# A two-layer diffusion backbone step: splitting the first FFN weights during the output projection, other FFN pass sizes in layer 1, and the gate transposes at the end

## The chip, the cores and the metric

The kernel runs on one core of one Trainium2 chip. The metric is the device time of one execution in microseconds (us). The core has five engines that work side by side: TensorE (PE, matmuls, with its weight loads as PEld), VectorE (DVE), ScalarE (ACT), GpSimd (POOL) and SyncE (SP), which here issues all DMAs in one queue, in order. Every engine runs its instructions in a fixed order and waits on semaphores; an instruction that waits holds up all that stand behind it on its engine.

## The reference

One inference step of two layers over 1152 tokens (1024 latent, 128 context) of width 1024. In each layer an input projection feeds three mixers (latent attention, an mLSTM and a gated linear recurrence), and then:

```
mix = jnp.concatenate([a_out, m_out, g_out], axis=-1) @ lp['w_out']
x = layernorm(ALPHA * x + g1 * mix, lp['ln1_g'], lp['ln1_b'])
h2 = x * (1 + sc2) + sh2
gate, up = jnp.split(h2 @ lp['w_ffn_in'], 2, axis=-1)
x = layernorm(ALPHA * x + g2 * ((jax.nn.silu(gate) * up) @ lp['w_ffn_out']), lp['ln2_g'], lp['ln2_b'])
```

The FFN is 2816 wide, which is 22 blocks of 128. The vectors sh, sc and g come from `silu(c) @ w_mod + b_mod`, for each layer and for two kinds of token. All of it is float32.

## The kernel before

**Number format.** Every matmul is done in three products of split operands: a value is held as hi (an ACT cast, L150, for weights L145) and lo (source minus hi, L151 or L146, on DVE or POOL), and hi·hi, lo·hi and hi·lo are added in PSUM (L155 to L157). A "unit" is a weight tile of 128x1024: a DMA into a raw buffer (L144), hi (L145), lo (L146). The raw buffers are a ring, `r_raw`, and a load waits until the buffer that it takes is free.

**Phases.** Each of the layers 0 and 1 runs phase A (input projection), B (mixers), C (output projection), D (FFN). Tokens are worked in 9 tiles of 128, n=0 to 8.

- *Phase C* takes a tile n through 48 matmuls of 128x512. DVE multiplies by the gate row (L1394) and adds ALPHA·x (L1395), where x was loaded at L1385 into a ring of three buffers, `rx` (in layer 1 DVE first multiplies and adds rows to x, L1387 and L1388). Then comes the layer norm: DVE statistics (L1322 to L1324), a power on POOL (L1325), DVE (L1333), an ACT scaling (L1334). `next_h` transposes the tile on PE (8 transposes, L1342), empties the two banks by ACT (L1347) and DVE (L1349), splits the result into `hhi` and `hlo`, and stores three differences of its quarters in DRAM, `sex` (L1354 to L1359). The normed x goes to DRAM as well, `sx` (L1399, or L1403 behind two POOL operations, L1401 and L1402, in layer 0).
- *`ffn_in`* computes gate and up in seven products p1 to p7 for each of the 22 blocks, a Strassen scheme over 2x2 quarters (matmuls at L1449). Each product has two parts q (token tiles 0 to 4 and 5 to 8). p1, p5, p2 and p3 use hhi and hlo; p6, p7 and p4 use three tiles `ex` that are loaded back from sex (L1536) and split (L1537 and L1538). A block's weights are loaded (L1454, L1455), summed on DVE (L1466, L1472 to L1474) and split into seven pairs. The ring of x and other buffers of phase C are given back at its end, and the ex tiles take memory that phase C has held.
- *`ffn_out`* works in three passes over the 22 blocks: 9, 8 and 5 blocks in both layers (`PASSES`). In each pass a tile n loads its hidden values (L1596) and runs 6 matmuls of 128x512 for each block: 54, 48 and 30. Pass 0 leaves its sum in `acc`, pass 1 adds (L1613), multiplies by the gate (POOL, L1618) and adds ALPHA·x (DVE, L1619), where x, `xr`, was loaded at L1600 into a buffer of `r_raw`. Pass 2 adds the rest (L1615 on DVE, L1616 on DVE or POOL), and the layer norm follows. In layer 1 the last rows (L1634, L1635) and the store of the output (L1636) come behind it. The units of passes 0 and 1 are kept in the memory of hhi and hlo (`home`, nine slots), those of pass 2 in five more (`tail`). In layer 0, passes 0 and 1 also compute next layer's modulation, three vectors a tile (`mod_gemv`, L211 to L213: a load into `r_raw`, and two DVE operations of 128x1024), and `gsave` (L225 to L227) transposes two gates on PE and stores them through one buffer, `gT`.

**Order.** A scheduler decides in which order the instructions stand on each engine. It knows the program's dependencies and a model of the durations; on the chip the order is then fixed.

## Time and profile before

| | us |
|---|---|
| three runs: median (lowest, highest) | 3640.34 (3639.33, 3640.81) |
| the profiled execution, its own time | 3641.28 |
| its span, first to last instruction | 3639.5 |
| PE busy in the span | 3405.9 (94%) |
| DVE, POOL, ACT busy | 2264.8, 1988.8, 1635.7 |
| output projection of layer 0, last matmul | 1033.9 |
| output projection of layer 1, last matmul | 2810.6 |
| FFN output of layer 0, pass 1 into pass 2 | about 1765 |
| FFN output of layer 1, first and last matmul | about 3324 and 3621.7 |

The times in the rows below are us from the start of the span. In a timeline row the bracket at the end is how long the engine was idle just before, and what it waited for. The granted clock of PE (PEclk) is 1.00 at its higher level, 2.4 GHz, and 0.50 at its lower one, 1.2 GHz.

### The profile page before, as it was taken

What the parts mean: (1) busy time and instruction counts of PE and PEld (TensorE: products, weight loads), DVE (VectorE), ACT (ScalarE), POOL (GpSimd) and SP (SyncE); (2) the same over time, 40 slices, a digit from 0 to 9 for tenths busy, and PEclk for the clock granted to TensorE, in tenths of its full rate; (3) what the DMA queues carried; (4) which work ended last, traced back from release to release, by engine and by line L of the source; (5) the groups of instructions that cost most, each with busy time, mean ns of one, the idle gap of its engine ahead of it and who ended that gap; (6) DMA issues with size and microseconds to landing.
All of it is one profiled execution on the core that took longest, in us unless ns stands there. A gap on an engine that the chain in (4) does not pass through costs nothing. (4 is left out here: it accounts for less than half of the span.)

```text
span 3639.5 us, 56085 instructions
## 1 busy us (share of the span) xinstructions
PE 3405.9 (94%) x20556; PEld 3034.6 (83%) x20556; DVE 2264.8 (62%) x4492; ACT 1635.7 (45%) x2877; POOL 1988.8 (55%) x1745
## 2 busy tenths in 40 slices
PE   7999987999989999999889989989999999999997
PEld 7998875776779999988689888877767899998875
DVE  6868878555674444487775678765558544443246
ACT  4264564887343333312272636577853433333211
POOL 3455566777665555401453556567863555552176
PEclk9899976999989999999999999789999999999998
DMA  6212153002352222375422021401044322224222
GB/s 244 72 40 43 39 167 100 18 21 81 121 160 85 85 85 85 111 252 179 156 79 62 30 45 34 137 25 25 22 132 139 110 73 73 73 74 139 94 99 80
DMA packets 331272, 335.77 MB, mean 92 GB/s; under 512 B 191458, under 2 KB 270386, under 8 KB 330996
## 3 DMA queue, kind: packets, MB, share of 16 engines
q1 hardware_dynamic: 330996, 332.19, 29.5%
q8 instruction: 161, 2.64, 0.3%
q14 instruction: 115, 0.94, 0.1%
HBM read 263.54 MB, written 68.56 MB: 91 GB/s over the span
## 5 line engine op out<-in xcount | busy, mean ns | idle before, releaser
L151 POOL TENSOR_TENSOR t<-t,t 128x512 fp32r<-128x512 f32 (+3 forms) x318 | 437.8, 1378 | 374.8 <-ACT t L150 374.4
L150 ACT CAST t<-t 128x512 fp32r<-128x512 f32 (+5 forms) x404 | 270.7, 673 | 698.0 <-PE bank L1449 278.7
L1449 PE MATMUL bank<-hhi,t 128*128 128x256 f32 (+1 forms) x2816 | 570.8, 295 | 12.4 <-DVE t L1349 11.5
L155 PE MATMUL bank<-hhi,t 128*128 128x384 f32 (+1 forms) x1220 | 455.1, 378 | 19.2 <-ACT t L150 5.1
L157 PE MATMUL bank<-hhi,t 128*128 128x384 f32 (+1 forms) x1220 | 460.0, 378 | 8.8 <-DVE t L151 8.8
L1449 PEld LDWEIGHTS bank<-hhi,t 128*128 128x128 f32 x2816 | 456.2, 189 | 13.6 <-ACT t L150 12.3
L156 PE MATMUL bank<-hlo,t 128*128 128x384 f32 (+1 forms) x1220 | 460.9, 378 | 4.9 <-POOL hlo L151 4.1
L1187 POOL TENSOR_TENSOR t<-t,t 128x512 fp32r<-128x512 f32 (+1 forms) x304 | 383.3, 1281 | 125.4 <-ACT t L1186 103.0
L1449 PE MATMUL bank<-t,t 128*128 128x320 f32 (+1 forms) x3168 | 434.2, 297 | 2.3 <-DVE t L1507 1.7
L1449 PEld LDWEIGHTS bank<-t,t 128*128 128x128 f32 x3168 | 427.9, 190 | 3.7 <-DVE t L1507 1.9
L1449 PE MATMUL bank<-hlo,t 128*128 128x320 f32 (+1 forms) x1408 | 415.2, 295 | 0.0
L155 PE MATMUL bank<-t,hhi 128*128 128x256 f32 (+3 forms) x1232 | 386.8, 315 | 12.1 <-DVE t L1107 5.4
L156 PE MATMUL bank<-t,hhi 128*128 128x256 f32 (+3 forms) x1232 | 388.0, 315 | 4.3 <-POOL t L146 4.3
L157 PE MATMUL bank<-t,hlo 128*128 128x256 f32 (+3 forms) x1232 | 388.4, 316 | 0.3 <-POOL hlo L151 0.3
L155 PEld LDWEIGHTS bank<-hhi,t 128*128 128x128 f32 x1220 | 237.9, 196 | 57.3 <-ACT t L150 6.7
L1137 DVE TENSOR_REDUCE t<-bank 128x1 f32<-128x384 f32 (+1 forms) x400 | 203.9, 538 | 122.6 <-PE bank L1136 119.5
L157 PEld LDWEIGHTS bank<-hhi,t 128*128 128x128 f32 x1220 | 240.1, 197 | 39.2 <-DVE t L151 12.1
L156 PEld LDWEIGHTS bank<-hlo,t 128*128 128x128 f32 x1220 | 239.6, 196 | 34.7 <-POOL hlo L151 5.1
L1449 PEld LDWEIGHTS bank<-hlo,t 128*128 128x128 f32 x1408 | 265.4, 188 | 0.3 <-issue 0.2
L155 PEld LDWEIGHTS bank<-t,hhi 128*128 128x128 f32 x1232 | 239.8, 195 | 30.2 <-DVE t L1107 5.6
L213 DVE SCALAR_TENSOR_TENSOR t<-t,t 128x1024 bf16<-128x1024 f32 x176 | 239.3, 1359 | 40.6 <-DMA t<-in_w_mod_dram 31.6
L156 PEld LDWEIGHTS bank<-t,hhi 128*128 128x128 f32 x1232 | 240.4, 195 | 20.1 <-POOL t L146 4.7
(355 smaller groups left out, 7329.1 us busy)
## 6 DMA issues: line engine op xcount, KB each, us to landing
t<-in_w_mod_dram SPq DMA_DIRECT2D x96, 512.0 KB
t<-in_w_ffn_in_dram SPq DMA_DIRECT2D x88, 512.0 KB
t<-in_w_ffn_out_dram SPq DMA_DIRECT2D x44, 512.0 KB
t<-in_w_in_dram SPq DMA_DIRECT2D x40, 512.0 KB
shid<-t SPq DMA_DIRECT2D x88, 160.0 KB
sx<-t SPq DMA_DIRECT2D x27, 512.0 KB
t<-sx SPq DMA_DIRECT2D x27, 512.0 KB
shid<-t SPq DMA_DIRECT2D x88, 128.0 KB
```

The source lines that it names most:

```text
L150: self.nc.scalar.copy(hi, src)
L151: (eng or self.nc.gpsimd).tensor_tensor(lo, src, hi.bitcast(F32), op=ALU.subtract)
L155: mm(ps, a[0], b[0], start=first, stop=False)
L156: mm(ps, a[0], b[1], start=False, stop=False)
L157: mm(ps, a[1], b[0], start=False, stop=last)
L213: nc.vector.scalar_tensor_tensor(junk, raw, 1.0, cB[s], op0=ALU.mult, op1=ALU.mult, accum_out=self.modfm[:, l, j, s:s + 1])
L1137: V.tensor_reduce(nm[:, i, b:b + 1] if i < 8 else nm[:, i, 3:4], ps, axis=AX.X, op=ALU.max, negate=True)
L1187: G.tensor_tensor(pl, e, ph.bitcast(F32), op=ALU.subtract)
L1449: mm(ps, a[x][:, k * P:(k + 1) * P], view(y, k, n0, n1), start=first and k == 0 and i == 0, stop=k == 3 and i == 2, skip_group_check=True)
```

## The change

The first block's weights of `ffn_in` were loaded, summed and split behind the output projection; now a generator, `ffn_weights`, is taken one step further at each of the tiles n=5 to 8 of phase C, so that a11, the first sum sA, a12 and sC are split there. For that phase C and `ffn_in` share the rings `r_raw` (four buffers instead of phase C's own three), `rS` and four of the nine pairs of `rA`, and phase C gives up memory: `rx` has two buffers instead of three, `ru` one instead of two. In `next_h` the split into hhi and hlo stands ahead of the last two differences. In layer 1 the FFN output passes have 5, 8 and 9 blocks; pass 0 has its units in `home[0:5]`, pass 1 in `home[5:9]` and four of `tail`, pass 2 in all of `home`. In layer 0 the modulation vectors, 48 in all, were worked three a tile, 27 in pass 0 and the rest at the tiles n=0 to 6 of pass 1; now pass 1 has three a tile up to n=4 and two a tile for n=5 to 7. Both `gsave` come at the end of `ffn_out`.

```diff
-PASSES = ((0, 9), (9, 17), (17, KF))
+PASSES = (((0, 9), (9, 17), (17, KF)), ((0, 5), (5, 13), (13, KF)))
+PRE = 4
...
+        V.tensor_tensor(e[:, 1], b22, b12, op=ALU.subtract)
+        V.tensor_tensor(b12, b12, b11, op=ALU.subtract)
+        self.split(self.hhi[:, :, c], self.hlo[:, :, c], t3, V if n == 8 else None)
+        V.tensor_tensor(e[:, 0], b22, b12, op=ALU.subtract)
+        V.tensor_tensor(e[:, 2], b21, e[:, 0], op=ALU.subtract)
...
-            self.r_raw = z.ring(3, [P, U])
...
-            rx = z.ring(3, [P, D])
+            rx = z.ring(2, [P, D])
...
-            rt, ru = z.ring(2, [P, D]), z.ring(2, [P, D])
+            rt, ru = z.ring(2, [P, D]), z.ring(1, [P, D])
...
+                if n == 4:
+                    gen = self.ffn_weights(l, 0, rS, rA)
+                elif n > 4:
+                    next(gen)
...
+            self.r_raw = z.ring(4, [P, U])
...
+                rS = zi.ring(3, [P, 512])
+                rA = Ring([[zi([P, 512], F32R) for _ in range(2)] for _ in range(PRE)])
...
+    def ffn_weights(self, l, j, rS, rA):
...
+        def sp(src):
+            s = rA.next()
+            self.split(s[0], s[1], src, V if j == 0 else G)
+            out.append(s)
+
+        V.tensor_tensor(sA, a21, a22, op=ALU.add)
+        for src in (a11, sA):
+            sp(src)
+            yield out
+        V.tensor_tensor(sB, sA, a11, op=ALU.subtract)
+        V.tensor_tensor(sC, a12, sB, op=ALU.subtract)
+        V.tensor_tensor(a21, a11, a21, op=ALU.subtract)
+        for src in (a12, sC, sB, a22, a21):
+            sp(src)
+            yield out
...
-        tail = [(z([P, U], F32R), z([P, U], F32R)) for _ in range(PASSES[2][1] - PASSES[2][0])]
+        tail = [(z([P, U], F32R), z([P, U], F32R)) for _ in range(4 if last else 5)]
...
+        slots = [home[0:5], home[5:9] + tail, home] if last else [home, home, tail]
+        for i, (j0, j1) in enumerate(PASSES[l]):
+            w = [self.unit(ins["w_ffn_out"][l, j * P:(j + 1) * P, :], slot=slots[i][j - j0],
+                           eng=V if i == 0 or not last and i == 1 or last and i == 2 and j - j0 > 4 else G) for j in range(j0, j1)]
...
-                for g in (16, 40):
-                    self.gsave(1, g, r_t.next())
...
+                now = 0 if i == 1 and n == 8 else 2 if i == 1 and n > 4 else 3
+                for m in mods[:now]:
...
+        if not last:
+            for g in (16, 40):
+                self.gsave(1, g, r_t.next())
```

In the changed file the lines of `next_h` stand one further down, those of phase C five to six (L1395 becomes L1401), those of `ffn_out` some twelve (L1618 becomes L1630).

**First place: ACT behind the output projection of layer 1.** Rows of the order on ACT, before the change. The casts of shape 128x4x320 are hi of the ex tiles (L1537) and wait for their loads; L1334 is the norm's scaling, L1347 empties a bank of transposes, L150 into hhi follows it.

```order
L1334 ACTIVATE t_25063<-t_25063,t_25087 128x1024
L150 CAST t_26054<-t_25938 128x512
L1347 ACTIVATE t_25071<-bank_68,t_25095,t_25091 128x128 x4
L1537 CAST t_25950<-t_25954 128x4x320
L150 CAST hhi_76<-t_25071 128x8x128
L1334 ACTIVATE t_25059<-t_25059,t_25083 128x1024
L1537 CAST t_25958<-t_25962 128x4x320
L1347 ACTIVATE t_25067<-bank_66,t_25095,t_25091 128x128 x4
```

The same stretch of the changed kernel, where these are L1548, L1335, L1348 and L151:

```order
L1548 CAST t_25961<-t_25965 128x4x320
L1335 ACTIVATE t_25081<-t_25081,t_25101 128x1024
L1335 ACTIVATE t_25085<-t_25085,t_25105 128x1024
L151 CAST hhi_76<-t_25089 128x8x128
L1348 ACTIVATE t_25089<-bank_66,t_25113,t_25109 128x128 x4
L1548 CAST t_25969<-t_25973 128x4x320
L151 CAST hhi_76<-t_25089 128x8x128
L1335 ACTIVATE t_25081<-t_25081,t_25101 128x1024
L1348 ACTIVATE t_25089<-bank_68,t_25113,t_25109 128x128 x4
L151 CAST hhi_76<-t_25089 128x8x128
L1548 CAST t_25977<-t_25981 128x4x320
L1348 ACTIVATE t_25089<-bank_66,t_25113,t_25109 128x128 x4
```

Before, one scaling (n=8) stands behind the first ex cast; now those of n=6 and 7 do, that of n=8 stands behind the second, and emptying the bank of n=8 behind the third.

**Second place: POOL from pass 1 into pass 2 of layer 0's FFN output.** Before the change; L146 is lo of a unit of pass 2, in the order of its raw buffers u0, u1, u4, u2, u3.

```order
L146 TENSOR_TENSOR t_14740<-t_9766,t_14736 128x1024
L1618 TENSOR_TENSOR t_14776<-t_14776,t_14780 128x1024
L146 TENSOR_TENSOR t_14748<-t_9770,t_14744 128x1024
L146 TENSOR_TENSOR t_14772<-t_9766,t_14768 128x1024
L1618 TENSOR_TENSOR t_14776<-t_14776,t_14780 128x1024
L146 TENSOR_TENSOR t_14756<-t_9758,t_14752 128x1024
L146 TENSOR_TENSOR t_14764<-t_9762,t_14760 128x1024
```

After it (L147 and L1630), in the order u1, u0, u2, u4, u3:

```order
L147 TENSOR_TENSOR t_14726<-t_8774,t_14722 128x1024
L147 TENSOR_TENSOR t_14718<-t_8770,t_14714 128x1024
L147 TENSOR_TENSOR t_14734<-t_8762,t_14730 128x1024
L1630 TENSOR_TENSOR t_14754<-t_14754,t_14758 128x1024
L147 TENSOR_TENSOR t_14750<-t_8770,t_14746 128x1024
L147 TENSOR_TENSOR t_14742<-t_8766,t_14738 128x1024
```

Before, u0 stood ahead of the multiplication of n=7, and u1 and u4 between it and that of n=8; now that of n=7 stands ahead of all units, and u1, u0 and u2 ahead of that of n=8.

**Third place: SP from pass 1 into pass 2 of layer 1's FFN output.** Before the change; L1600 is the load of xr (here n=8), L144 a unit of pass 2, L1596 a tile's hidden values.

```order
L1600 DMA t_25938<-sx_92 128x1024
...
L1596 DMA t_30846<-shid_119 128x640
L144 DMA t_25942<-in_w_ffn_out_dram 128x1024
...
L144 DMA t_25942<-in_w_ffn_out_dram 128x1024
L1596 DMA t_30850<-shid_119 128x640
L144 DMA t_25946<-in_w_ffn_out_dram 128x1024
L1596 DMA t_30846<-shid_119 128x640
L144 DMA t_25934<-in_w_ffn_out_dram 128x1024
L1596 DMA t_30850<-shid_119 128x640
L144 DMA t_25938<-in_w_ffn_out_dram 128x1024
```

After it (L1612, L145 and L1608), with nine units in the order u0, u4, u1, u8, u5, u2, u6, u3, u7:

```order
L1612 DMA t_24917<-sx_92 128x1024
...
L1608 DMA t_30799<-shid_122 128x1152
L145 DMA t_24921<-in_w_ffn_out_dram 128x1024 x2
L1608 DMA t_30803<-shid_122 128x1152
L145 DMA t_24925<-in_w_ffn_out_dram 128x1024
L145 DMA t_24921<-in_w_ffn_out_dram 128x1024
L145 DMA t_24925<-in_w_ffn_out_dram 128x1024
L1608 DMA t_30799<-shid_122 128x1152
L145 DMA t_24913<-in_w_ffn_out_dram 128x1024 x2
L1608 DMA t_30803<-shid_122 128x1152
L145 DMA t_24917<-in_w_ffn_out_dram 128x1024 x2
```

In both, the last load of a unit takes the buffer that held xr of n=8 (t_25938 before, t_24917 now). Before, one of five units did; now two of nine do, one behind the other.

## Rows read from the trace of the kernel before

**Rows 1.** The page, part 1: busy time, share and instructions.

```profile
PE 3405.9 (94%) x20556; PEld 3034.6 (83%) x20556; DVE 2264.8 (62%) x4492; ACT 1635.7 (45%) x2877; POOL 1988.8 (55%) x1745
```

**Rows 2.** Windows: stretch, length, busy time (instructions) by engine, granted clock, DMA share, GB/s.

```profile
1010.00:1034.00 24.00, 24.00 (x113) 19.56 (x112) 16.52 (x33) 8.76 (x14) 17.52 (x10) 1.00 0.45 136
2750.00:2770.00 20.00, 20.00 (x96) 16.36 (x95) 18.97 (x32) 7.30 (x13) 7.39 (x4) 1.00 0.41 122
1725.00:1765.00 40.00, 36.56 (x158) 28.90 (x156) 38.45 (x52) 3.88 (x4) 9.67 (x4) 1.00 0.61 202
1765.00:1795.00 30.00, 18.45 (x55) 12.53 (x55) 12.24 (x8) 6.38 (x7) 18.21 (x9) 0.83 0.30 103
3323.90:3525.00 201.10, 199.89 (x865) 163.60 (x866) 64.77 (x50) 36.26 (x43) 64.78 (x27) 0.99 0.30 99
3525.00:3570.00 45.00, 32.67 (x109) 24.49 (x108) 14.85 (x12) 8.15 (x9) 21.25 (x9) 0.81 0.23 81
3570.00:3610.00 40.00, 40.00 (x178) 33.14 (x177) 30.09 (x50) 8.96 (x10) 38.79 (x31) 1.00 0.26 88
3610.00:3622.00 12.00, 9.55 (x41) 7.25 (x39) 11.56 (x16) 2.67 (x3) 9.44 (x8) 1.00 0.23 87
```

**Rows 3.** Timeline of PE around the ends of both output projections.

```profile
1033.91 0.40 PE L157 MATMUL bank<-t,hlo 128*128 128x512 f32 x1
...
1045.41 1.97 PE L1342 MATMUL bank<-ident,t 128*128 128x128 f32 x8 [8.46 <-ACT t L1334]
1054.42 0.60 PE L1449 MATMUL bank<-hhi,t 128*128 128x320 f32 x1 [7.04 <-DVE t L1349]
...
2810.58 0.40 PE L157 MATMUL bank<-t,hlo 128*128 128x512 f32 x1
...
2829.51 0.61 PE L1449 MATMUL bank<-hhi,t 128*128 128x320 f32 x1 [4.49 <-DVE t L1349]
```

**Rows 4.** Timelines of SP and ACT: first ex load and its cast, both layers.

```profile
1034.34 0.57 SPq L1536 DMA_DIRECT2D t<-sex  x1
...
1039.91 1.26 ACT L1537 CAST t<-t 128x1280 fp32r<-128x1280 f32 x1 [3.16 <-DMA t<-sex]
...
2811.20 1.42 SPq L1536 DMA_DIRECT2D t<-sex  x2
...
2819.65 1.26 ACT L1537 CAST t<-t 128x1280 fp32r<-128x1280 f32 x1 [4.93 <-DMA t<-sex]
```

**Rows 5.** Timeline of DVE behind layer 0's output projection.

```profile
1041.20 1.49 DVE L1538 TENSOR_TENSOR t<-t,t 128x1280 fp32r<-128x1280 f32 x1 [1.98 <-ACT t L1537]
...
1046.97 3.28 DVE L1538 TENSOR_TENSOR t<-t,t 128x1280 fp32r<-128x1280 f32 x1 [2.89 <-ACT t L1537]
1050.18 2.82 DVE L1466 TENSOR_TENSOR t<-t 128x512 f32<-128x512 f32 x1
1052.92 1.35 DVE L1349 TENSOR_SCALAR t<-bank,t,t 128x128 f32<-128x128 f32 x4
```

**Rows 6.** Timelines of DVE, SP and POOL in layer 0's FFN output, pass 1 into 2.

```profile
1778.41 3.34 DVE L1619 SCALAR_TENSOR_TENSOR t<-t,t 128x1024 f32<-128x1024 f32 x1 [2.33 <-POOL t L1618]
...
1781.78 0.34 SPq L144 DMA_DIRECT2D t<-in_w_ffn_out_dram  x1
...
1786.78 2.36 POOL L146 TENSOR_TENSOR t<-t,t 128x1024 fp32r<-128x1024 f32 x1 [6.11 <-ACT t L145]
```

**Rows 7.** Timeline of DVE in layer 0's FFN output, the last modulation operation.

```profile
1761.12 1.22 DVE L213 SCALAR_TENSOR_TENSOR t<-t,t 128x1024 bf16<-128x1024 f32 x1
```

**Rows 8.** Timelines of DVE, SP and PE in layer 1's FFN output, pass 1 into 2.

```profile
3556.60 1.23 DVE L1619 SCALAR_TENSOR_TENSOR t<-t,t 128x1024 f32<-128x1024 f32 x1 [2.48 <-POOL t L1618]
...
3557.85 0.33 SPq L144 DMA_DIRECT2D t<-in_w_ffn_out_dram  x1
...
3562.32 2.01 PE L155 MATMUL bank<-t,t 128*128 128x512 f32 x4 [3.05 <-ACT t L145]
```

**Rows 9.** Timeline of DVE behind the last matmul.

```profile
3630.43 0.68 DVE L1615 TENSOR_TENSOR t<-bank,t 128x512 f32<-128x512 f32 x1
```

More of the change, by code (lines that the diff above doesn't have):

```diff
@@ L1350, in next_h, with phase_c @@
         t3 = tmp.rearrange("p (k t) -> p k t", k=KD)
-        if e is not None:
-            V, G = nc.vector, nc.gpsimd
-            b11, b12, b21, b22 = [t3[:, 4 * i:4 * i + 4, 64 * j:64 * j + 64] for i in range(2) for j in range(2)]
-            V.tensor_tensor(e[:, 1], b22, b12, op=ALU.subtract)
-            V.tensor_tensor(b12, b12, b11, op=ALU.subtract)
-            V.tensor_tensor(e[:, 0], b22, b12, op=ALU.subtract)
-            V.tensor_tensor(e[:, 2], b21, e[:, 0], op=ALU.subtract)
-            for i in range(3):
-                nc.sync.dma_start(self.s_ex[i][:, :, n * 64:(n + 1) * 64], e[:, i])
-        self.split(self.hhi[:, :, c], self.hlo[:, :, c], t3, nc.vector if e is not None and n == 8 else None)
-    def phase_c(self, l):
+        if e is None:
+            self.split(self.hhi[:, :, c], self.hlo[:, :, c], t3)
+            return
+        V = nc.vector
+        b11, b12, b21, b22 = [t3[:, 4 * i:4 * i + 4, 64 * j:64 * j + 64] for i in range(2) for j in range(2)]
+        V.tensor_tensor(e[:, 1], b22, b12, op=ALU.subtract)
[3 more added lines that the diff above has]
+        V.tensor_tensor(e[:, 2], b21, e[:, 0], op=ALU.subtract)
+        for i in range(3):
+            nc.sync.dma_start(self.s_ex[i][:, :, n * 64:(n + 1) * 64], e[:, i])
+    def phase_c(self, l, rS, rA):
         nc, ins = self.nc, self.ins
@@ L1419, in ffn_in @@
         r5, r3 = z.ring(2, [P, T2]), z.ring(2, [P, T2])
-        rS = z.ring(3, [P, 512])
-        rA = Ring([[z([P, 512], F32R) for _ in range(2)] for _ in range(9)])
+        rA.tiles.extend([z([P, 512], F32R) for _ in range(2)] for _ in range(9 - PRE))
         X, Y, Z, W = [[self.bank[2 * i], self.bank[2 * i + 1]] for i in range(4)]
@@ L1482, in block @@
             s5, u3 = r5.next(), r3.next()
-            i = [j < b for a, b in PASSES].index(True)
-            jj = j - PASSES[i][0]
+            i = [j < b for a, b in PASSES[l]].index(True)
+            jj = j - PASSES[l][i][0]
             def ps(bk, q):
@@ L1523, in p7 @@
                     n0, n1 = PARTS[q]
[L1524 removed]
+                    nc.sync.dma_start(self.s_h[l][i][n0:n1, :, jj, 64 * h:64 * h + 64].rearrange("n p t -> p n t"),
                                       t[:, c].rearrange("p (n t) -> p n t", t=64))
             return (p1, p5, p2, p3, p6, p4, p7)
[L1529 to L1531 removed]
+        for w in gen:
+            pass
         for q, (n0, n1) in enumerate(PARTS):
@@ L1548, in ffn_in @@
                 if (s, q) == (4, 1) and more:
-                    rest()
+                    for w in gen:
+                        pass
             if mods and j % 2 == 1:
@@ L1580, in ffn_out @@
         home = [[a[:, i * U:(i + 1) * U] for a in flat] for i in range(9)]
-        for i, (j0, j1) in enumerate(PASSES):
-            w = [self.unit(ins["w_ffn_out"][l, j * P:(j + 1) * P, :], slot=(tail if i == 2 else home)[j - j0],
-                           eng=V if i < 2 else G) for j in range(j0, j1)]
+        slots = [home[0:5], home[5:9] + tail, home] if last else [home, home, tail]
+        for i, (j0, j1) in enumerate(PASSES[l]):
+            w = [self.unit(ins["w_ffn_out"][l, j * P:(j + 1) * P, :], slot=slots[i][j - j0],
+                           eng=V if i == 0 or not last and i == 1 or last and i == 2 and j - j0 > 4 else G) for j in range(j0, j1)]
             if i == 2 and last:
@@ L1623, in ffn_out @@
                         self.mod_bias(1, m - 7, 8)
-                mods = mods[3:]
+                mods = mods[now:]
                 if i < 2:
```

66 lines of the change are left out of this document (25 added, 41 removed).

## The prediction

> **What bounds the kernel now.** The page's busy times come first: PE is busy 94% of the span, no other engine over 62% [rows 1]. So the time is PE's work plus the stretches where PE stands still or runs at its lower clock. I looked for those in the windows, stage by stage, then in the timelines for what ends each wait.
>
> A 128x512 matmul at the full clock takes 201.1/865 = 0.2325 us [rows 2]. With that the windows show what a stage loses. Layer 0's FFN output: 1765 to 1795 holds 55 matmuls, 12.8 us of 30, so 17.2 lost; the 40 us ahead hold 158, 3.3 lost. Layer 1's: 3525 to 3570 holds 109, 25.3 of 45, so 19.7 lost; the whole of it, 1188 matmuls or 276.2 us, takes 297.8 (3323.9 to 3621.7), so 21.6 lost. Then 17.8 us pass to the span's end at 3639.5. From the last matmul of the output projection to p5 of the first FFN block it is 1054.42 − 1033.91 = 20.5 us in layer 0 and 2829.51 − 2810.58 = 18.9 in layer 1 [rows 3], with little but p1 (12 matmuls) and transposes in them. The change touches all five places.
>
> **Layer 1's FFN output, passes 5, 8, 9: −28.5.** Before, the last unit of pass 2 takes the buffer of xr n=8: L1619 frees it (3556.60 to 3557.8), SP loads (3557.85), and PE starts on it at 3562.32 [rows 8], 4.5 us from load to use, with lo still to come. PE has nothing else to do, since pass 2 has five units. Now it has nine. PE works tiles 0 and 1 over four banks in the order in which units arrive: the seven that come ahead of u3 and u7 are 7·12·0.2325 = 19.5 us of work. Let E be the end of pass 1. In the new order the multiplication by the gate of n=8 stands behind u2's lo; L1631 ends near E+4.5, u3's load, hi and lo take until E+12 (4.5 and 2.4 and the queue), needed at E+19.5; u7 takes the same buffer behind u3's lo, E+18, needed at E+22.3. So about 20 of the 21.6 go; the start of pass 0 keeps its wait.
>
> The tail: pass 2 now has 54 matmuls a tile, 12.6 us. Before it had 30, 7.0 us, and POOL was busy 38.79 of 40 us [rows 2]. Behind the last matmul DVE came to the last L1615 only at 3630.43 [rows 9], 8.7 us late, since DVE and POOL were behind; from there 9.1 us lead to the end. Now that L1615 should stand right behind the last matmul: 17.8 − 9.3 = 8.5. Sum −28.5. Ends: −18 (u7 late by 6 us, half of the tail) and −30.
>
> **Layer 0's FFN output: −4.** The worst wait is u3's: L1619 of n=8 at 1778.41 takes 3.34 us, the load is issued at 1781.78, lo runs from 1786.78 for 2.36, to 1789.1 [rows 6]. Pass 1 ends at about 1765, so that is E+24. The modulation vectors are only moved, and the last ones end later: at 1762.3 before [rows 7], behind L1631 of n=7 and near 1766 after. That frees u2's buffer; with 5.0 us from load to lo [rows 6] and POOL's queue its lo ends near 1774.5, then the gate multiplication of n=8 (2.4) and L1631 (1.2) near 1778, u3's load to lo 5.0 and 2.4: 1785.5, some 3.6 earlier. Ends: +2 (late by DVE, which is full ahead of it, 38.45 of 40 us [rows 2]) and −14 (the vectors do end by E, and each step is 2 us shorter).
>
> **Both gsave behind pass 2: +1.** Two transposes and copies now stand at the start of layer 1's phase A, the second behind the first one's store, since gT is one buffer. Nothing shows them there; between 0 and half an ex load, 3 us [rows 4].
>
> **Layer 0, C into D: −4.** Before, p5 waits until L1349 (n=8) has emptied its bank, behind an ex lo of 3.28 us and a weight sum of 2.82 [rows 5]. In the new order both stand elsewhere, but the first ex lo (ends 1042.7) and two sums still stand ahead of the norm of n=8. From 1042.7 on: sums and differences 2.8, POOL's hlo of n=7 and the power 1.5, scaling 1.3: transposes at about 1049 (before 1045.4). They take 2.0 [rows 3], then L1349 1.35 [rows 5]: p5 at 1052.6 instead of 1054.4, with p6's 12 matmuls (1.8 us) done before it. Ends: −7, and +7 if DVE runs late (last rival).
>
> **Layer 1, C into D: +13.** Here the order is worse. With two buffers in rx the tiles go in pairs, and the transposes of n=6, 7 and 8 all come behind the last matmul. On ACT the scalings of n=6 and 7 stand behind the first ex cast, that of n=8 behind the second, and emptying its bank behind the third. The ex tiles lie in memory of x and of the normed tile of n=8, so the three loads follow one another. From the last matmul: load 5.6, as in layer 0 [rows 4], hi 1.3, two scalings, store of n=6 (about 3, estimated as half a load) frees the tile for n=8 at 11.5; L1400 and L1401 free x at 14.5; second load to 20, hi and scaling to 22.7, store to 26; third load to 31.5, hi and lo: p4 at about 34.3, p5 right behind it. Before, p5 came at 18.9: 15.4 later, less p6's 1.8 and some small waits: +13. Ends: +4 (the loads overlap) and +28 (loads of 8.4 us, as here before [rows 4], and DVE late, which is full in this phase, 18.97 of 20 us [rows 2]).
>
> The Trainium skill (DMA: Bandwidth & Descriptors, the fixed and variable cost of a DMA) puts a transfer at about 2.0 us plus its bytes over 436 GB/s. For an ex load of 0.66 MB an estimate by it is 3.5 us; this case's trace shows 5.6 and 8.4. By the page this term would be about +7, and the whole 3612.
>
> **Sum.** −28.5 − 4 + 1 − 4 + 13 = −22.5 against the profiled execution's own time of 3641.3 (1.8 above its span): 3618.8. The median of the runs is 0.9 lower, so **3618**.
>
> **Rivals.**
> - *Layer 1's stall is only moved* (chance 0.12). u3 and u7 come through one buffer, two loads in a row behind xr n=8, and SP's queue is in order: u4, behind u0's lo, holds up u1. For it: with loads of 8.4 us u7 is there at E+27 or later, and the tiles' last L1615 wait for it. Against: unit loads there took 4.5 us with hi [rows 8]. Price: 12 us, 3630.
> - *Layer 0 gains all that its order allows* (0.10): −14 instead of −4, 3608.
> - *Layer 1 loses nothing between C and D* (0.10): the loads land while DVE works on n=7 and 8 anyway. 3605.
> - *DVE and POOL hold each other up in layer 0's phase C* (0.07): the moved operations run while POOL works 17.52 of 24 us [rows 2]; on DVE the same ex lo took 1.49 alone and 3.28 beside POOL [rows 5]. Twelve operations with 1 to 2 us more each are 12 to 24 on DVE, which had 7.5 of 24 free. The norm of n=8 would come up to 11 us late: p5 at +7 instead of −4, 3629. The Trainium skill (SBUF — State Buffer, SBUF: two separate sides) says that a DVE instruction with two SBUF inputs and a GpSimd instruction take one port pair in turn, the later one waiting for the whole of the other. By that rule the 3.28 is the normal case here.
> - *Slower* (0.07): the pairs make layer 1's phase C itself wait. A pair's loop on DVE is: four L1400 and two L1401, 5.1 us; statistics 2.6; the wait for the next x, which is loaded only behind L1401 (5.6 to 8.4 less what DVE does meanwhile); four row operations of 1.2; transposes' emptying, norm and scaling some 5; a store, 3. That is 21 to 25 us, where PE needs 22.3 a pair; four banks cover 11 us of lateness. To undo the gains it must cost 22.5 us over four pairs, so it decides where the loop passes 22.3 + 11/4 + 22.5/4 = 31 us. Twice the waits for x and store do that: then 3649.
>
> **How the numbers follow.** The forecast has 0.54, with 3609 to 3627 from its own terms. The range leaves out two in ten: 3602 to 3634, which holds the four smaller rivals alone but not two bad ones together. A measurement of this kernel tells about 0.2%, 7.3 us, from no change: below 3633 has 0.82; within it 0.11, from two of the bad rivals together and the small end of the pairs' loop; slower 0.07.
>
> **What the changed profile would show.** In layer 1's FFN output no wait over 2 us between passes 1 and 2, and the last L1627 within 1 us of the last matmul; if u3 or u7 is late, PE waits on ACT L146 or POOL L147 some 20 us into pass 2. In layer 0 u3's lo ends near 1785, with the last modulation operation near 1766. Behind layer 1's output projection ACT waits three times for sex, and p4 starts some 34 us after the last 128x512 matmul; if it stands at 20, that term is wrong. The prediction fails if PE waits for DVE inside layer 1's phase C, or if the first matmuls of pass 0 in layer 1 wait for the hidden values of n=1, whose load now stands behind four more units.

## The result

The changed kernel is slower: 3676.7 us (median; 3668.91 to 3678.06) against 3640.6 (3639.33 to 3646.56), a ratio on record of 1.0086, interval [1.0065, 1.0107] (the two medians divided give 1.0099). The forecast was 3618, within 3602 to 3634.

Part 1 of the changed kernel's page, which answers to [rows 1], shows almost the same work in a span of 3675.7 instead of 3639.5 us. PE works the same 20556 matmuls; 24.5 us of the difference are idle time of PE, and 11.7 us are matmuls that took longer.

```profile
PE 3417.6 (93%) x20556; PEld 3042.6 (83%) x20556; DVE 2268.9 (62%) x4484; ACT 1635.7 (45%) x2877; POOL 2004.9 (55%) x1753
```

To place the loss I cut both spans at matmuls that both have: the last of 96x512 in phase B ("B's end": 926.11 before, 923.07 after), the last 128x512 of phase C, and the first and last 128x512 of the FFN output. In us:

| stretch | before | after | change | forecast |
|---|---|---|---|---|
| start to B's end, layer 0 | 926.1 | 923.1 | −3.0 | 0 |
| layer 0, B's end to FFN output | 623.0 | 650.3 | +27.3 | −4 |
| of it, to phase C's last matmul | 107.8 | 127.9 | +20.1 | 0 |
| layer 0, FFN output | 300.0 | 312.3 | +12.3 | −4 |
| from there to layer 1's B's end | 852.1 | 853.0 | +0.8 | +1 |
| layer 1, B's end to FFN output | 623.6 | 639.3 | +15.7 | +13 |
| of it, to phase C's last matmul | 109.3 | 113.0 | +3.7 | 0 |
| layer 1, FFN output | 296.4 | 289.2 | −7.3 | −20 |
| last matmul to the end | 18.2 | 8.6 | −9.6 | −8.5 |

The changes add up to 36.2, the difference of the spans. In other kernels that leave phases A and B as they are, "from there to layer 1's B's end" took 851 to 866, so a change of that stretch is not read as an effect of anything. All stretches are read from one traced execution of each kernel.

**Phase C of layer 0.** Windows from B's end to the last matmul, first of before, then of after (columns as in [rows 2]):

```profile
926.10:1033.90 107.80, 107.80 (x493) 87.15 (x492) 67.94 (x130) 33.95 (x54) 72.64 (x38) 1.00 0.44 134
```

```profile
923.10:1050.90 127.80, 112.89 (x493) 88.96 (x492) 91.69 (x139) 37.15 (x60) 69.67 (x37) 0.97 0.38 118
```

PE never stood still there before. After, it works as many matmuls, is idle for 14.9 us, and has a granted clock of 0.97 instead of 1.00. Its busy time is 5.1 us longer. The timeline of DVE at the start of that stretch, before and then after:

```profile
933.32 0.48 DVE L1313 TENSOR_TENSOR t<-modfm,cols 128x16 f32<-128x16 f32 x1 [10.81 <-PE bank L1257]
...
943.93 0.18 DVE L1212 RECIPROCAL t<-t 128x4 f32<-128x4 f32 x1 [0.77 <-DMA t<-sdn]
944.02 1.25 DVE L1322 BATCH_NORM_STATS2 t<-t 128x6 f32<-128x512 f32 x2
```

```profile
944.47 1.29 DVE L1400 TENSOR_TENSOR t<-bank,t 128x512 f32<-128x512 f32 x2 [4.53 <-DMA sdn<-t]
945.79 1.22 DVE L1401 SCALAR_TENSOR_TENSOR t<-t,t 128x1024 f32<-128x1024 f32 x1
950.89 0.69 DVE L1443 TENSOR_TENSOR t<-t 128x512 f32<-128x512 f32 x1 [3.87 <-DMA t<-in_w_ffn_in_dram]
951.50 0.17 DVE L1213 RECIPROCAL t<-t 128x4 f32<-128x4 f32 x1
951.61 0.69 DVE L1449 TENSOR_TENSOR t<-t,t 128x512 f32<-128x512 f32 x1
958.18 0.18 DVE L1314 TENSOR_TENSOR t<-modfm,cols 128x16 f32<-128x16 f32 x1 [5.87 <-POOL t L1220]
958.27 0.17 DVE L1315 TENSOR_TENSOR t<-modfm,cols 128x16 f32<-128x16 f32 x1
958.36 1.28 DVE L1323 BATCH_NORM_STATS2 t<-t 128x6 f32<-128x512 f32 x2
```

L1323 (L1322 before) is the statistics of tile n=0, 14.3 us later (17.4, counted from B's end). Three waits stand ahead of it on DVE, and none of the three was there before (the long wait of before, for PE, ended 10.7 us ahead of the statistics): for a store of phase B (`sdn`), for a load of FFN weights whose sum (L1443, the second of its kind, so block 1's) the scheduler put here, and for POOL's last product of phase B (L1220), in front of the write to the small tile Gs (L1314). The three hang together: the reciprocal (L1213), whose result L1220 multiplies, stands behind that sum, at 951.50 instead of 943.93. From then on the norms are late, and PE waits at their transposes. The first row is the longest of these waits; the others come behind phase C, in layer 0 and in layer 1:

```profile
1012.94 1.38 PE L1343 MATMUL bank<-ident,t 128*128 128x128 f32 x6 [3.16 <-ACT t L1335]
...
1060.94 0.64 PE L1489 MATMUL bank<-t,t 128*128 128x320 f32 x1 [7.00 <-ACT t L1548]
1065.76 3.30 PE L1489 MATMUL bank<-t,t 128*128 128x320 f32 x11 [4.19 <-DVE t L1549]
1072.09 1.97 PE L1343 MATMUL bank<-ident,t 128*128 128x128 f32 x8 [3.03 <-ACT t L1335]
1075.58 0.64 PE L1489 MATMUL bank<-hhi,t 128*128 128x320 f32 x1 [1.52 <-DVE t L1350]
...
2858.49 0.63 PE L1489 MATMUL bank<-t,t 128*128 128x320 f32 x1 [6.46 <-ACT t L1548]
2874.34 1.97 PE L1343 MATMUL bank<-ident,t 128*128 128x128 f32 x8 [7.73 <-ACT t L1335]
2882.86 0.64 PE L1489 MATMUL bank<-t,t 128*128 128x320 f32 x1 [6.56 <-ACT t L1548]
```

The other rows answer to [rows 3]: p5 starts 24.7 us behind layer 0's last 128x512 (1050.92), before 20.5; layer 1's last stands at 2851.64, and PE has three long waits in a row, two for the cast of an ex load and between them one for the scaling of n=8, which stands behind the second cast; p4 starts 31.2 us behind the last matmul. In layer 0 the norm of n=8 is late, since on DVE three splits of block 0's weights (L152) and a sum (L1447) stand in front of its second gate product (L1400), which starts 6.6 us behind the last matmul:

```profile
1050.49 5.47 DVE L152 TENSOR_TENSOR t<-t,t 128x512 fp32r<-128x512 f32 x3 [1.81 <-ACT t L151]
1055.89 1.74 DVE L1447 TENSOR_TENSOR t<-t,t 128x512 f32<-128x512 f32 x1
1057.55 0.68 DVE L1400 TENSOR_TENSOR t<-bank,t 128x512 f32<-128x512 f32 x1
```

In layer 1's phase C (+3.7) the longest wait of PE is one for DVE:

```profile
2777.86 0.80 PE L156 MATMUL bank<-t,hhi 128*128 128x512 f32 x1 [4.79 <-DVE t L1400]
```

**FFN output of layer 0.** PE's two waits between passes 1 and 2, the last modulation vectors on DVE, the units' first load and u3's lo (timelines of PE, DVE, SP and POOL, as in [rows 6, 7]):

```profile
1809.73 2.08 PE L156 MATMUL bank<-t,t 128*128 128x512 f32 x4 [11.78 <-ACT t L146]
1823.28 1.19 PE L156 MATMUL bank<-t,t 128*128 128x512 f32 x4 [2.12 <-ACT t L146]
...
1797.82 1.23 DVE L214 SCALAR_TENSOR_TENSOR t<-t,t 128x1024 bf16<-128x1024 f32 x1 [3.66 <-DMA t<-in_w_mod_dram]
...
1805.14 1.21 DVE L214 SCALAR_TENSOR_TENSOR t<-t,t 128x1024 bf16<-128x1024 f32 x1
...
1800.83 5.88 SPq L145 DMA_DIRECT2D t<-in_w_ffn_out_dram  x3
...
1823.30 2.36 POOL L147 TENSOR_TENSOR t<-t,t 128x1024 fp32r<-128x1024 f32 x1 [2.40 <-ACT t L146]
```

PE stops at 1798. The last vectors wait for their own loads and end at 1806.4, and the units' loads start only 2.9 us behind the stop.

**FFN output of layer 1**, timelines of PE, DVE and SP (as [rows 8]), and the tail (as [rows 9]):

```profile
3548.26 1.22 PE L156 MATMUL bank<-hhi,t 128*128 128x512 f32 x2 [5.00 <-ACT hhi L146]
3561.74 2.07 PE L156 MATMUL bank<-hhi,t 128*128 128x512 f32 x4 [4.58 <-ACT hhi L146]
...
3549.19 2.56 DVE L147 TENSOR_TENSOR hlo<-t,hhi 128x1024 fp32r<-128x1024 f32 x1 [3.69 <-ACT hhi L146]
3551.68 0.68 DVE L1625 TENSOR_TENSOR t<-bank,t 128x512 f32<-128x512 f32 x1
3555.92 1.23 DVE L1631 SCALAR_TENSOR_TENSOR t<-t,t 128x1024 f32<-128x1024 f32 x1 [2.30 <-POOL t L1630]
...
3557.17 7.30 SPq L145 DMA_DIRECT2D t<-in_w_ffn_out_dram  x2
...
3667.56 0.69 DVE L1627 TENSOR_TENSOR t<-bank,t 128x512 f32<-128x512 f32 x1 [4.04 <-PE bank L158]
```

Pass 1 ends near 3541. PE waits 5.00 us for u2 and 4.58 for u3, whose load stands behind n=8's L1631, and that behind L1625, which stands behind the lo of another unit, u8 (L147). The last L1627 follows the last matmul (3667.13) by 0.4 us, where it was 9 us before.

### The profile page after: what moved, and what is told of

It is laid out like the page before. It is cut to its first block, busy times and chain, and to the rows that moved or that the text cites. A ratio compares the mean times of both kernels' runs of the same rounds, so it can differ in the third digit from the quotient of the medians.

```text
span 3675.7 us, 56123 instructions
## 1 busy us (share of the span) xinstructions
PE 3417.6 (93%) x20556; PEld 3042.6 (83%) x20556; DVE 2268.9 (62%) x4484; ACT 1635.7 (45%) x2877; POOL 2004.9 (55%) x1753
## 4 chain that ended last, share of the span: by engine, by line
PE 50%; DVE 8%; DMA 4%; POOL 3%; issue 3%; ACT 3%; SPq 0%; DVEq 0%; ACTq 0%; POOLq 0%
PE bank L1489 26%; PE bank L156 5%; PE bank L157 5%; PE bank L158 5%; DVE t L214 1%; PE bank L624 1%; DMA t<-in_w_ffn_out_dram 1%; PE bank L1183 1%; PE bank L1258 1%; PE bank L1256 1%; PE bank L1184 1%; PE bank L1185 1%; PE bank L1257 1%; PE bank L1137 1%; POOL t L1630 1%
## 5 line engine op out<-in xcount | busy, mean ns | idle before, releaser
L152 POOL TENSOR_TENSOR t<-t,t 128x512 fp32r<-128x512 f32 (+3 forms) x318 | 431.9, 1360 | 374.9 <-ACT t L151 373.2
L1489 PE MATMUL bank<-hhi,t 128*128 128x320 f32 (+1 forms) x2816 | 572.9, 296 | 1.5 <-DVE t L1350 1.5
L151 ACT CAST t<-t 128x512 fp32r<-128x512 f32 (+5 forms) x404 | 269.9, 673 | 669.7 <-PE bank L1489 282.0
L156 PE MATMUL bank<-hhi,t 128*128 128x384 f32 (+1 forms) x1238 | 465.9, 382 | 34.0 <-ACT hhi L146 9.6
L158 PE MATMUL bank<-hhi,t 128*128 128x384 f32 (+1 forms) x1238 | 465.5, 377 | 5.1 <-DVE t L152 5.1
L1489 PE MATMUL bank<-hlo,t 128*128 128x256 f32 (+1 forms) x1408 | 416.9, 296 | 0.6 <-DVE hlo L152 0.6
L156 PE MATMUL bank<-t,hhi 128*128 128x256 f32 (+3 forms) x1232 | 392.1, 319 | 18.8 <-DVE t L1400 6.3
L157 PE MATMUL bank<-t,hhi 128*128 128x256 f32 (+3 forms) x1232 | 391.8, 318 | 4.6 <-POOL t L147 4.6
L157 PEld LDWEIGHTS bank<-t,hhi 128*128 128x128 f32 x1232 | 244.5, 198 | 20.7 <-POOL t L147 5.0
```

What stands on the lines that cost most here:

```text
L151: self.nc.scalar.copy(hi, src)
L152: (eng or self.nc.gpsimd).tensor_tensor(lo, src, hi.bitcast(F32), op=ALU.subtract)
L156: mm(ps, a[0], b[0], start=first, stop=False)
L157: mm(ps, a[0], b[1], start=False, stop=False)
L158: mm(ps, a[1], b[0], start=False, stop=last)
L1489: mm(ps, a[x][:, k * P:(k + 1) * P], view(y, k, n0, n1), start=first and k == 0 and i == 0, stop=k == 3 and i == 2, skip_group_check=True)
```

## The experiments

Ratios are to the kernel before, run on the same chip at the same time (medians there 3644 to 3650). "C" is layer 0 from B's end to phase C's last matmul, "0" and "1" the stretch of each layer from B's end to the FFN output (before: C 107.8, 0 623.0, 1 623.6; in the kernels that leave phases B to D alone C is 107.8, 0 lies at 624 to 627, 1 at 625 to 628, so costs of these two stretches against before are uncertain by some 4 us). The traced execution lies up to 11 us from its kernel's median: those of e2 and e15 are the slowest of their runs, that of e17 is the fastest. Of each edit the main lines are shown; `...` stands for the others.

**Parts of the change alone.** e1 is before with the new passes:

```diff
-PASSES = ((0, 9), (9, 17), (17, KF))
+PASSES = (((0, 9), (9, 17), (17, KF)), ((0, 5), (5, 13), (13, KF)))
...
```

> The kernel before with only the passes of layer 1's FFN output changed to 5, 8, 9 blocks. Theory (the traces of before and after put side by side): the wait between passes 1 and 2 stays, since PE takes pass 2's units in the order u0, u1, u2, u3 and u2 and u3 come late; only the tail and some 5 us of PE are gained. 3640.6 - 10 - 5 = about 3626. Rival (the prediction's term): about 3612, and the missing gain in the changed kernel came from what the other edits did to the order.

3635.45 us, 0.9971 [0.9952, 0.9989]: the passes gain 10.9 us (before had 3646.34 beside it), somewhat over a third of the 28.5 that I forecast.

e2 is before with the smaller rings:

```diff
-            rx = z.ring(3, [P, D])
+            rx = z.ring(2, [P, D])
...
-            rt, ru = z.ring(2, [P, D]), z.ring(2, [P, D])
+            rt, ru = z.ring(2, [P, D]), z.ring(1, [P, D])
```

> The kernel before with only rx of two buffers instead of three and ru of one instead of two; nothing is split early. Theory: phase C waits for x in both layers, +12 us in layer 0 and +4 or more in layer 1 by the changed kernel's idle rows, 3657 or more. Rival: the early splits on DVE, in turn with POOL, make phase C late, and the rings alone cost nothing: 3641.

3656.12, 1.0028 [1.0013, 1.0043]; C 111.0, 0 628.7, 1 631.7: they cost 5.6 and 8.1 us, 3.2 and 4.9 of it in phase C, and not all of 27.3 and 15.7.

e3 is before with the new places of vectors and gates:

```diff
-                for m in mods[:3]:
+                now = 0 if i == 1 and n == 8 else 2 if i == 1 and n > 4 else 3
+                for m in mods[:now]:
...
```

> The kernel before with only the modulation vectors rearranged in pass 1 of layer 0's FFN output and both gate transposes at the end. Theory: the last vectors' loads go through the same raw buffers as pass 2's units, which then start some 8 us later; with the start of pass 0 this costs about 12 us in all: 3653. Rival: the stall at the start of that phase and the late units came from the shared raw ring of the early split, and this edit is worth between 0 and -4: 3637 to 3641.

3643.06, 1.0001 [0.9988, 1.0013]. In total nothing, but layer 0's FFN output took 305.4 (300.0), with one wait of 11.94 us for ACT L145 like the changed kernel's.

e4 is the early split with its rings alone (the changed kernel with the old passes and places; the new order in `next_h` is still in it, and no run takes that apart).

> The changed kernel with passes and modulation as before: only the early split, with its shared rings and the smaller rx and ru. Theory: all of the loss in phases C and C into D, 17 + 7 + 4 + 10 = +38, 3678. Rival: a part of it belongs to the other two edits, by the order that the scheduler then finds: below 3665.

3683.27, 1.0106 [1.0079, 1.0133]; C 125.7, 0 647.1, 1 639.1; layer 0's FFN output 307.6, of which 7.4 us are waits at its start, where gates and hidden values come behind the last FFN operations on DVE. So the early split with its rings makes the loss by itself.

**Layer 1's FFN output.** e5 is e1 with PE working pass 2's units in the order in which they are loaded; e6 is e1 with pass 2's first five units loaded at the tiles n=0 to 4 of pass 1; e7 does that in layer 0 too, in pass 0.

```diff
+                    ks = [0, 4, 1, 8, 5, 2, 6, 3, 7] if last and i == 2 else list(range(j1 - j0))
-                    for k in range(j1 - j0):
+                    for k in ks:
...
```

The second cut is e7's; in e6 the condition is `last and i == 1`.

```diff
...
+                if i == (1 if last else 0) and n < 5:
+                    j = PASSES[l][2][0] + n
+                    early.append(self.unit(ins["w_ffn_out"][l, j * P:(j + 1) * P, :], slot=slots[2][n], eng=V if last else G))
...
```

> The kernel before with the passes 5, 8, 9, and PE told to take the nine units of pass 2 in the order in which their loads are issued (u0, u4, u1, u8, u5, u2, u6, u3, u7) instead of u0 to u8. Theory: the wait between passes 1 and 2 is there because PE takes u2 third and u3 fourth, while these come last but a few; in the order of arrival the two waits of about 5 us and the low clock behind them go, 8 to 10 us under the kernel with the passes alone. Rival: the raw buffers' chain is too slow in any order, the units of one buffer come 7 us apart: no difference to the kernel with the passes alone.

> The kernel before with the passes 5, 8, 9, and the first five units of pass 2 of layer 1 loaded and split during pass 1, one behind each of the tiles n=0 to 4, since their memory is free since pass 0. Theory: the chain over xr n=8 is what makes the wait, so no wait is left between passes 1 and 2: about 15 us under the kernel with the passes alone, 0.993 of the kernel before. Rival: DVE and the raw ring are too busy in pass 1, and the wait is moved into it: the same as the passes alone.

> As the kernel with early units in layer 1, and in layer 0 the five units of pass 2 are loaded during pass 0 (lo on POOL, which is idle there). Theory: the 17 us lost between passes 1 and 2 of layer 0 are the same chain, so they go too, less some 3: 0.989 of the kernel before. Rival: the raw ring of four has three modulation loads a tile in it, and a fifth load a tile stalls DVE's modulation work, which is the bound of both passes: 0.993 or more.

Layer 1's FFN output: e1 292.4, e5 282.5, e6 276.4, and 1188·0.2325 = 276.2 is PE almost without a wait, by the stretch in [rows 2] (e7 has 274). Layer 0's in e7: 282.7. Times: e5 3634.59, 0.9952 [0.9932, 0.9971]; e6 3622.49, 0.9917 [0.9897, 0.9938]; e7 **3599.65**, 0.9859 [0.9842, 0.9877]. e7 has no part of the early split and beats both kernels.

**What costs phase C.** e8 is e4 with the full rings (`rx` 3, `ru` 2) and two pairs split early instead of four.

```diff
-PRE = 4
+PRE = 2
...
-                if n == 4:
+                if n == 6:
```

> The early split alone, with rx of three and ru of two as before, and with two of the seven pairs (a11 and sA) split in phase C, at n=7 and 8, since the memory of four pairs is needed for the rings. Theory: the smaller rings are what costs most in phase C, together with the order that follows from them: phase C without waits, C into D a few us shorter than before: 0.999 to 1.001 of the kernel before. Rival: the early loads and sums on DVE and the raw ring shared with phase C's own weights cost it: 1.005 or more.

3679.08, 1.0083 [1.0055, 1.0110]; C 120.9, 0 642.8, 1 632.1. That is less than e4 (125.7, 647.1, 639.1), but with the full rings C still loses 13.1 us: the rings are not the main cause.

e9 is the changed kernel with Gs and Hs in memory of their own, e10 with block 1's raw buffers taken only from phase D on, e11 with both and e7's early units, e12 is e8 with both.

```diff
+        self.cGs, self.cHs = t(self.pp, [P, 8, 2], name="cGs"), t(self.pp, [P, 8, 2], name="cHs")
...
-            Gs, Hs = self.combo_tiles(z)
+            Gs, Hs = self.cGs, self.cHs
```

```diff
-            self.r_raw = z.ring(4, [P, U])
+            self.own = z.ring(2, [P, U])
...
```

> The changed kernel, with the two small tiles of phase C's normalisation (Gs, Hs, 64 bytes a partition each) in memory that nothing else uses. In the changed kernel DVE waits 5.87 us at L1314, the write to Gs, for POOL's last product of phase B (L1220), with the statistics of row n=0 (958.36 us; 944.02 before) right behind it; layer 1 the same, 5.85 us. Theory (the new tiles moved Gs onto memory that phase B uses, and this wait is most of the 20 us that each phase C lost): n=0's statistics stand some 6 us or more earlier, the stretch from phase B's last 512-column matmul to phase C's last shrinks from 127.9 to about 115 us in layer 0, and by some 10 us in layer 1, total about 3655 us, 1.004 of the kernel before. Rival (the split's work and the smaller rings are what phase C waits for; the wait at L1314 only hides it): the stretch stays within 4 us of 127.9, total 3670 to 3677.

> The changed kernel, with the four buffers of raw weights split: two from before phase C on (block 0's), two only from phase D on, so that block 1's first sum can't be worked ahead of phase C's row 0. In the changed kernel DVE stands 3.87 us at that sum (950.89 us) with phase B's reciprocal and row 0's statistics behind it. Theory (the wait of Gs for POOL is what matters; this one only moves it): the stretch of phase C goes from 127.9 to some 123 us, total about 3668 us, 1.0075 of before. Rival (the early sums on DVE are the whole cause): the stretch goes to 112 us or less, total 3650 or less.

> The changed kernel with both of these, and with the weights of the first five blocks of each layer's last output pass loaded during the pass before (as in the kernel that gave 3599.65). Theory: phase C as in the kernel before plus about 5 us in each layer, layer 0's output passes about 288 us (282.7 there, and 5.4 for the gate matrices' new order), layer 1's 276 us: total about 3622 us, 0.994 of before, still behind 3599.65. Rival (with the waits gone the split gives its gain at the start of phase D): total 3590 us or less.

> The early split alone (the kernel with the full rings, rx 3 and ru 2, and two of block 0's pairs ready before phase D, which took 3679.08 us, 1.0083 of before), with Gs and Hs and the raw buffers in memory of their own as in the two kernels above. Theory (memory that is waited for is the cost, not the work of the split): each phase C within 4 us of the kernel before's 107.8 us, total 3640 to 3652 us, 1.000 to 1.003 of before. Rival (the split's work in phase C costs it by itself): the stretch stays at 116 us or more, total 3665 or more.

e9: 3689.86, 1.0116 [1.0095, 1.0138], C 126.1. e10: 3672.53, 1.0078 [1.0060, 1.0096], C 121.1. e11: 3637.47, 0.9979 [0.9966, 0.9993], C 121.2. e12: 3681.91, 1.0101 [1.0084, 1.0119], C 118.6. The theories of e9 and e12 fall as I had put them: C hardly moved. e10 comes out near its theory: without block 1's sum ahead of n=0, C is 6.8 us shorter (0: 640.6), so some 13 of the 20 us remain. e11's total is above its theory. DVE's timeline in e9 says why Gs alone was not enough:

```profile
960.87 1.29 DVE L1324 BATCH_NORM_STATS2 t<-t 128x6 f32<-128x512 f32 x2 [5.93 <-POOL t L1221]
```

The wait for POOL did not go; it stands at the next small tile, that of the statistics. So I added up all tiles' sizes. Phase B's last u and rB (L1220 multiplies them) lie 92 to 101 KB up the stack. Phase C's tiles ended at 86 KB before and end at 104 KB after, since the shared buffers lie below them; ru, the statistics, Gs, Hs and the exchange tile now lie on u and rB.

e13 is the kernel *before* with 18 KB of unused memory below phase C's tiles, e14 with 8 KB:

```diff
+            z([P, 4608])
             self.r_raw = z.ring(3, [P, U])
```

> The kernel before with one addition: 18 KB a partition of memory that nothing uses, taken ahead of all of phase C's left-hand tiles. No instruction is added and no buffer is smaller; it only moves the tiles. Counted up from the sizes of the tiles, phase B's last product u and its last reciprocals rB lie at 92 to 101 KB from the start of the stack, phase C's tiles end at 86 KB in the kernel before and at 104 KB in the changed one, where the product's tile ru, the statistics, Gs, Hs and the exchange tile lie on u and rB; the 18 KB put them at the same place. Theory (the place in memory is most of what each phase C lost: row 0 can't be normalised before phase B's last row is done): the stretch from phase B's last 512-column matmul to phase C's last goes from 107.8 us to 115 to 121 us in layer 0, about as much again is lost in layer 1, total 3654 to 3664 us, 1.004 to 1.0065 of before. Rival (the split's work and small rings are the cost, the place is not): 107.8 within 3 us, total within 0.1% of before.

> The same with 8 KB: the small tiles then lie at 88 KB, below u and rB; only the second exchange tile touches u. Theory (it is u and rB that are waited for): layer 0's stretch within 4 us of 107.8, total 3640 to 3650 us, less than 1.002 of before. Rival (any place above the old one costs): about half of what 18 KB cost.

e13: 3673.09, 1.0074 [1.0054, 1.0095]; C 117.5, 0 634.8, 1 641.1. e14: 3637.69, 0.9978 [0.9961, 0.9994]; C 107.9, 0 624.7, 1 621.8. With not one instruction more on any engine, the place costs nearly what the whole change did (and more than the theory's total), and 10 KB lower it costs nothing. DVE's timeline of e13 has two of the changed kernel's three waits ahead of n=0, shorter, and its window of C the idle PE:

```profile
944.48 1.88 DVE L1395 TENSOR_TENSOR t<-bank,t 128x512 f32<-128x512 f32 x3 [2.34 <-DMA sri<-t]
...
949.82 0.18 DVE L1313 TENSOR_TENSOR t<-modfm,cols 128x16 f32<-128x16 f32 x1 [1.18 <-POOL t L1219]
```

```profile
919.20:1036.70 117.50, 109.94 (x494) 88.30 (x493) 78.50 (x130) 34.62 (x55) 70.95 (x38) 0.99 0.39 119
```

The scheduler knows that the tiles overlap, so the place shows in the order of the instructions too (L1313 stood ahead of n=0's gate products before and stands behind them in e13); what the order costs and what the waits cost, no run takes apart. In layer 1 the padding costs 17.4 us, but not where the theory has it: C is 107.4 there (109.3 before), though x of n=0 is multiplied by the rows 21 us behind B's end instead of 14. The loss lies behind C, from its last matmul to the FFN output (533.7 against 514.3), where PE waits for the cast of an ex load. Why the padding delays that load is not shown.

```profile
2841.42 0.64 PE L1450 MATMUL bank<-t,t 128*128 128x320 f32 x1 [11.39 <-ACT t L1538]
```

e15 is the changed kernel with phase B's u and rB in the other order, so that the last pair lies under the split weights, which are needed only from n=5 on; e16 adds the early units.

```diff
-            rU = Ring(rU + [z([P, T]) for _ in range(2)])
+            rU = Ring([z([P, T]) for _ in range(2)] + rU)
```

> The changed kernel, with phase B's two pairs of u and rB in the other order, so that the last ones lie at 30 to 39 KB, where phase C has block 0's split weights (needed from row 5 on), with 1.5 KB of padding behind these. Gs and the statistics then wait for nothing of phase B. Theory: row 0's statistics stand some 8 us earlier, layer 0's stretch goes from 127.9 to 114 to 119 us, layer 1 gains about as much, total 3655 to 3662 us, 1.004 to 1.006 of before. Rival (the work of the split costs phase C by itself): the stretch stays at 121 us or more, total 3668 or more.

> That, and the weights of the first five blocks of each layer's last output pass loaded during the pass before. Theory: the same phase C, layer 0's output passes about 298 us (as in the kernel with all three that took 3637.47 us), layer 1's 286 us, total about 3630 us, 0.996 of before. Rival: the split gives its gain once nothing holds it up, total 3600 us or less.

e15: 3676.18, 1.0082 [1.0058, 1.0105]; C 109.9, 0 639.5, 1 641.3. e16: 3652.45, 1.0009 [0.9993, 1.0025]; C 111.2. Phase C of layer 0 is back to 2 us above before, more than the theory asked, yet the totals of both are not what their theories say. Part is given back behind the last matmul: from there to the FFN output e15 takes 529.7 us (522.5 changed, 515.2 before), and n=8's transposes wait 10.41 us for its norm. Layer 1 gained nothing. My theory for it was that the rows of the norm's weights are needed first there, and that by the tiles' sizes they lie on phase B's last sums (78 to 86 KB). In e15 DVE still waits 5.0 us for block 1's sum ahead of n=0, and C is 109.9: that wait alone costs PE next to nothing; only where the tiles lie on u and rB too does it gain 6.8 us to take it away (e10).

e17 is e15 with phase C's tiles in another order (these rows lowest, x and the sum highest), e18 adds the early units.

```diff
...
+            rows = [z([P, D]) for _ in range(2)]
             gb = z([P, 2, D])
...
+            rx, rt = z.ring(2, [P, D]), z.ring(2, [P, D])
```

> The changed kernel with phase B's two pairs of u and rB in the other order, as before, and phase C's tiles in another order too: the rows of the norm's weights lowest (63 to 71 KB instead of 79 to 87 KB, where phase B's last sums lie), the tiles of x and of the sum highest. In layer 1 row 0 is multiplied by these rows first, and in the changed kernel that stands 24 us after phase B's last 512-column matmul, before 14 us. Theory (the place in memory is what costs layer 1 too): the stretch from phase B's last matmul to the first of the output passes goes from 639 to about 628 us in layer 1 (623.6 before) and stays at 640 us or less in layer 0 (650.3 changed, 623.0 before), total 3650 to 3660 us, 1.003 to 1.0055 of before. Rival (in layer 1 it is the split's own work): layer 1 stays at 636 us or more, total 3665 or more.

> That, and the weights of the first five blocks of each layer's last output pass loaded during the pass before. Theory: as e17 less 35 us, 3615 to 3625 us, 0.993 of before, behind the 3599.65 of the same early loads without the split. Rival: the split gains once its tiles lie well, 3598 us or less.

e17: 3650.94, 1.0013 [0.9999, 1.0026]; C 109.2, 0 640.9, 1 631.5. e18: 3634.31, 0.9965 [0.9950, 0.9981]. e17 differs from the changed kernel by the order of tiles (and 1.5 KB of padding) alone, and its ratio is 1.0013 instead of 1.0086. Not all of that can be put down to the tiles: of the 34.4 us between the two traced spans 17.2 lie in the two stretches, and 21.3 ahead of B's end of either layer, in stretches that differ from kernel to kernel anyway (from layer 0's FFN output to layer 1's B's end e18, with the same tiles, has 861.7 where e17 has 840.0); layer 1's FFN output lost 5.5. Layer 1's 631.5 lies between theory and rival, but the theory's reason is not it: C stays at 113.0 there, and the 8 us are won behind it (518.6 against 526.3; e18 519.1). In layer 0 the gain in C is again in part given back behind it, at n=8's transposes:

```profile
1059.01 1.97 PE L1343 MATMUL bank<-ident,t 128*128 128x128 f32 x8 [12.63 <-ACT t L1335]
```

With all its tiles placed better the change still does not gain; e18 falls short of its theory and is behind e7, which has no early split.

## Why the prediction was wrong

**The step that failed** is one that the sum lacks. I costed the early split by its operations on DVE, ACT and POOL, and by what they meet behind phase C's last matmul; phase C itself stood at nothing, except in two rivals, and nowhere did I ask what the shared buffers push the other tiles onto. That cost +20.1 us in layer 0's phase C. That the place of the tiles is the reason there is shown from both sides: padding alone costs 9.7 of C (e13), 10 KB less costs nothing (e14), and with u and rB moved away C falls from 127.9 to 109.9 (e15).

It is the largest error, not the only one. Forecast (−22.5) and measurement (+36.2) lie 58.7 us apart; phase C of both layers makes 23.8 of it, layer 0's FFN output 16.3, the stall in layer 1's FFN output 12.7, and layer 0's way from C into D 11.2; the rest is −5.3.

What stays open: over the whole stretches the place costs 11.8 and 17.4 us by e13, beside 27.3 and 15.7, and e17 takes back only 9.4 and 7.8, as part of what C wins in layer 0 is lost again behind it. The smaller rings cost 5.6 and 8.1 (e2), block 1's sum ahead of n=0 9.7 in layer 0 (e10). These do not simply add up. In layer 1 most of the loss, in e13 too, lies behind phase C, and why the place matters there no run shows.

- *Layer 0, C into D, −4.* It was +7.2: p5 24.7 us behind the last matmul, forecast 18.7. The transposes of n=8 stood 21.2 us behind it (1072.09), where I had 15: three splits and a sum, 7.2 us on DVE, stood ahead of n=8's second gate product, where I had only an ex lo and two sums ahead of the norm. That is work of the split. (The 3 us between p5's 4.2 and the 7.2 are within what this stretch varies by.)
- *Layer 1, C into D, +13.* It was +12.0, with three loads one after another as described: p4 at 31.2, forecast 34.3; the loads took 4.6 to 4.7 us from issue to cast, where I had 5.6. Its phase C lost 3.7 more, no more than with the smaller rings alone (e2: 4.9).
- *Layer 1's FFN output, −28.5.* It was −16.9. The tail was right (−9.6, forecast −8.5). The stall was mis-sized (−7.3, forecast −20), since I let PE work the units in the order of arrival. It works them u0 to u8, so it stood at u2 and u3, long before the 19.5 us of work that I counted had been done. u3 was also later than I had it: n=8's L1631 ends 16.1 us behind pass 1, forecast 4.5, and u3's hi is there at 20.7, where I had its lo done at 12. e5, with the order that I had assumed, gives 282.5, 6 us above PE without a wait, against the 1.6 forecast; e6 gives none. And the −7.3 is the best of six: the same passes gave −4 in e1 and between −1.7 and +0.1 in e9, e10, e15 and e17, so only the gain of the tail is sure.
- *Layer 0's FFN output, −4.* It was +12.3. I set the end of the last vectors near the end of pass 1; they end 8 us behind it, as they wait for loads, and u3's lo ends 27.7 us behind it, forecast 20.5. e3 shows 5.4 us from this. e4 has 7.6 from the early split, mostly at the start, for which I had no term.
- *The gates, +1*: not shown; the stretch that holds them (+0.8) varies by more than that.
- *The rivals.* The slower one, PE held by the pairs in layer 1's phase C, gave the right sign for another reason, in the other layer; the sign that it named, PE waiting for DVE inside layer 1's phase C, was there once (4.79 us), and that phase lost only 3.7. That DVE and POOL hold each other up in layer 0 happened, but as a consequence: DVE's 130 operations of C took 67.9 us before and 78.5 in e13, moved and not added.

## What to carry to other kernels

Memory that a stage takes earlier moves all tiles above it. List, before and after, what the first tiles of a stage lie on, and whether these are the last that the stage before lets go; on an engine that works in order one such wait can make all that follows start late. Test it by padding the old kernel: if an unused buffer costs as much as the change, the place is enough to make the loss. Then place the new kernel's tiles better and look at every stretch: here phase C came back, part of the loss moved behind it, and the kernel was no faster than before. And follow the consumer's order, not that of arrival, when counting how much work covers a load; here the cure was to load units a pass earlier (e7, 0.9859).
